# Evictions of q, k and V grouped by engine, V's blocks stored in another order, and GpSimd's row sums in pieces of 256 columns, in a gated pooling and forgetting-attention block

## The chip, the cores and the metric

The kernel runs on one core of a Trainium2 chip. A core has a matrix engine (TensorE, PE in the profile; its weight loads are shown apart as PEld), a vector engine (VectorE, DVE), an engine for activation functions and copies (ScalarE, ACT), a general one (GpSimd, POOL) and a queue engine that issues transfers (SyncE, SP). They run side by side and wait for each other by semaphores; each works through its own queue in order. The metric is the device time of one execution in microseconds (us).

## The reference

One decoder block on 1040 tokens (16 meta tokens in front of 1024), width 1024, eight heads of 64, everything in float32. Cut to what matters here:

```python
h = rmsnorm(x, norm_g)
proj = jnp.einsum('bld,dn->bln', h, w_in)
u_pool, z_pool, q, k, v, z_attn, f_logit, g_pool, g_attn = jnp.split(proj, _split_points(), axis=-1)
y_pool = causal_multiscale_pool(u_pool, pool_w, pool_scale) * jax.nn.silu(z_pool)
log_f = jax.nn.log_sigmoid((f_logit + b_forget).astype(jnp.float32))
y_attn = forgetting_attention(q, k, v, log_f).reshape(B, L, ATTN_WIDTH) * jax.nn.silu(z_attn)
merged = (jax.nn.sigmoid(g_pool) * jnp.einsum('blc,cd->bld', y_pool, w_up_pool)
          + jax.nn.sigmoid(g_attn) * jnp.einsum('blc,cd->bld', y_attn, w_up_attn))
return x + jnp.einsum('bld,de->ble', merged, w_out)
```

and a last RMS norm. Attention is causal softmax with a bias from the running sum of the log forget gates:

```python
s = jnp.einsum('bqhd,bkhd->bhqk', qb, kb).astype(jnp.float32) * scale
s = s + c[:, :, q0:q1, None] - c[:, :, None, :q1]
p = jax.nn.softmax(jnp.where(valid, s, -jnp.inf), axis=-1)
outs.append(jnp.einsum('bhqk,bkhd->bqhd', p.astype(vb.dtype), vb))
```

## The kernel before

**Numbers in two parts.** Matrix products keep nearly float32 accuracy: each operand is split into a high part in a rounded format (written by ACT as a copy) and a low part, the rest (a subtraction on DVE, or on GpSimd for weights), and a product is three matmuls: high by high, high by low, low by high (`g_mm3`, L166 to L172). So every projection that is used again leaves its PSUM bank twice: ACT copies the high part out, then DVE reads the same bank, subtracts the high part and writes the low one.

**Stages.** By the profile's times: to about 54 us the tokens are normed and transposed, and the projections q, k and v of head pair 0 are made, in pieces of the tokens (L479 to L510). To about 83 us the forget gates are made (`gates`, L519). To about 433 us runs attention. Then come a stage of recombined gate projections (L1209 to 1225), the two up-projections (from L1262) and the output product with the last norm (to L1454).

**Attention.** Eight heads stand in four pairs p = 0 to 3, with e = 0, 1 in a pair, and two halves of 512 queries: sixteen units. A unit goes over key blocks b of 128 keys: 5 blocks in the first half, 9 in the second. The keys are stored with the meta tokens in front; block 8 is the last 128 of the 1040 keys and counts only the 16 that block 7 has not. For a block, `qk` (L693) makes the scores in a PSUM bank, ACT and DVE take them out with the gate bias and mask (L713, L717) into a buffer S, and a running maximum is kept (L720, L722). When a unit's blocks are done, `maxes` finds the maxima. Then `soft` (L743) subtracts them (DVE, L749), takes the exponential (ACT, L750), splits it into ph (ACT, L757) and pl (DVE, L758), and GpSimd adds the exponentials of the blocks into acc (L761 to L766), from which the softmax's denominators are summed later. `av` (L770) multiplies two blocks behind by V (L774). The scores of the next unit are interleaved with the softmax of this one.

**Filling.** Between these steps, TensorE's queue is filled with projections of later pairs and with others that are stored to memory for later (class `Fill`). `F.pull(ns)` emits so many nanoseconds' worth of matmuls by a modelled cost, at each place where TensorE would otherwise wait. The generators `f_q`, `f_k` and `f_v` make q, k, V of the next pair with `q_piece` (L265), `k_piece` (L286), `v_piece` (L298) and `v_blocks` (L307). A weight chunk is loaded and split by `split_w` (L148; ACT at L157, GpSimd at L159).

**V.** `v_piece` lets ACT copy a projection to VT, channels by tokens (L301). `v_blocks` transposes blocks of 128 tokens of VT on TensorE (L312) into a bank, and takes them out into V[p, e], a tile of nine blocks with a place for the high and the low part (ACT L321, DVE L322), one head after the other. For pair 0 the blocks 6, 7, 8 and 0 are transposed after the gates (L819), for the other pairs in the filling (L815). As V is stored in the order 0 to 8, the blocks 6 to 8 and block 0 don't lie side by side, and each is an operation of its own.

**What sets the order.** TensorE's queue is in the order in which the program is written (`manual_schedule`, L89). Up to L517 all engines' queues keep the written order among themselves; behind that the framework's planner orders the queues of ACT, DVE, GpSimd and SP by the order written and by modelled times, and it can put later work into gaps of the earlier stage. `after` and `behind` (L113, L118) add an order by hand. Banks for scores and transposes come from `third` (L176): two of a pool and one of another in turn; banks for filling from a pool of two.

**Grouping.** `EVAC` (L42) says how the evictions of q and k are written: for pair 0 both heads together (all ACT copies, then all DVE subtractions), for the other pairs one head after the other. For q, the high part is written to both halves of the partitions.

Of the kernel before, what the change touches and what calls it, by code (L numbers as in the profile page):

```python
# [10 lines left out]
AF = mybir.ActivationFunctionType  # L11
# [11 lines left out]
KB = 128  # L23
NB = 9
# [16 lines left out]
NRC = 2  # L41
EVAC = (((0, 1),), ((0,), (1,)))  # L42
WARM = (4, 0)


def r32(ap):
    return ap.bitcast(F32)
# [7 lines left out]
def tile_hybrid_block(ctx, tc, x, meta, norm_g, w_in, b_forget, pool_w, pool_scale,  # L55
# [209 lines left out]
    def q_piece(p, w, c0, c1):  # L265
# [9 lines left out]

        for group in EVAC[p > 0]:
            for e in group:
                hi(e, rows(e)[0])
                if not p:
                    hi(e, rows(e)[1])  # L280
            for e in group:
                lo(e)
                if p:
                    hi(e, rows(e)[1])

    def k_piece(p, w, t0, t1):  # L286
        ps = yield from g_proj(w, t0, t1)
        for group in EVAC[p > 0]:
            for e in group:
                a, o = rows(e)  # L290
                for c, d in keys_of(t0, t1):
                    nc.scalar.activation(KA[p, e][a, d], ps[a, c], AF.Copy)
            for e in group:
                a, o = rows(e)
                for c, d in keys_of(t0, t1):
                    nc.vector.tensor_tensor(KA[p, e][o, d], ps[a, c], r32(KA[p, e][a, d]), op=ALU.subtract)  # L296

# [8 lines left out]

    def v_blocks(p, *parts):  # L307
        pt = (fill_bank() if spare[0] else third(psS, "ps")).rearrange("p (n e d) -> p n e d", e=2, d=64)
        n = 0
        for b0, b1 in parts:  # L310
            for b in range(b0, b1):
                nc.tensor.transpose(pt[:, n], VT[p][:, KS[b]:KS[b] + KB], ident)  # L312
                n += 1
                yield 109.0
        for e in range(2):
            n = 0
            for b0, b1 in parts:
                pv = pt[:, n:n + b1 - b0]
                n += b1 - b0
                vh = V[p, e][:, b0:b1, e, :]  # L320
                nc.scalar.activation(vh, pv[:, :, e, :], AF.Copy)  # L321
                nc.vector.tensor_tensor(V[p, e][:, b0:b1, 1 - e, :], pv[:, :, e, :], r32(vh), op=ALU.subtract)  # L322

# [12 lines left out]
    def f_v(p):  # L336
        w = w_chunk(COL_V + p * 128)
        VT[p] = gp.tile([128, L], F32, name="vt", tag="g")
        v_alloc(p)
        for c0, c1 in PIECES:  # L340
            yield from v_piece(p, w, c0, c1)
            if c0:
                yield from v_blocks(p, {384: (1, 3), 768: (3, 6)}[c0])

# [134 lines left out]
    for n, (kind, t0, t1) in enumerate(todo):  # L479
# [29 lines left out]
        if n in (4, 7, 10):  # L509
            run(v_blocks(0, (max(1, 2 * (n // 3) - 2), 2 * (n // 3))))  # L510
    G_.close()
# [161 lines left out]
    class Unit:  # L673
# [69 lines left out]
        def soft(self, b):  # L743
# [17 lines left out]
            if b == 1:  # L761
                if c0:
                    nc.gpsimd.tensor_copy(acc[:, :c0], S0[:, :c0])
                accs.append(nc.gpsimd.tensor_tensor(acc[:, c0:], S0[:, c0:], s[:, c0:], op=ALU.add))
            elif b > 1:
                accs.append(nc.gpsimd.tensor_tensor(acc[:kb, c0:], acc[:kb, c0:], s[:kb, c0:], op=ALU.add))  # L766
            if b >= LAG:
                self.av(b - LAG)

        def av(self, b):  # L770
            kb, c0 = self.kb[b], self.c0[b]
            v = V[self.p, self.e][:kb, b].rearrange("p j d -> p (j d)")
            for i, r in enumerate(self.P.pop(b)):
# [36 lines left out]
    def pair_fill(p):  # L810
        if p < 4:
            F.add(f"q{p}", f_q(p))
            F.add(f"k{p}", f_k(p), apart=True)
            F.add(f"v{p}", f_v(p), 4 * p - 2)
            F.add(f"v{p}", v_blocks(p, (6, 9), (0, 1)), 4 * p - 2, apart=True)  # L815

    pair_fill(1)
    gates()
    run(v_blocks(0, (6, 9), (0, 1)))  # L819
    def sums_at(i, tr):  # L820
# [662 lines left out]
```

## Time and profile before

| | us |
|---|---|
| median of three runs | 724.83 (724.09 to 724.98) |
| the profiled execution, whole | 725.36 |
| its span from the first to the last instruction | 723.7 |
| TensorE busy | 709.6 |
| VectorE busy | 515.9 |
| ScalarE busy | 425.4 |
| GpSimd busy | 333.1 |

A row of the timeline gives the start and length in us, the engine, the line of the kernel, the operation, output and inputs with their shapes, how many neighbouring instructions are merged in it, and in square brackets the time that the engine stood idle before it and what ended that. A row of waits gives who waited for whom, with the total in us, how often, and the longest. Matmuls are pipelined, so that the lengths of neighbours overlap; a group of eight has one start and one length.

### The profile page before, as it was taken

What the parts mean: (1) busy time and instruction counts of PE and PEld (TensorE: products, weight loads), DVE (VectorE), ACT (ScalarE), POOL (GpSimd) and SP (SyncE); (2) the same over time, 40 slices, a digit from 0 to 9 for tenths busy, and PEclk for the clock granted to TensorE, in tenths of its full rate; (3) what the DMA queues carried; (4) which work ended last, traced back from release to release, by engine and by line L of the source; (5) the groups of instructions that cost most, each with busy time, mean ns of one, the idle gap of its engine ahead of it and who ended that gap; (6) DMA issues with size and microseconds to landing.
All of it is one profiled execution on the core that took longest, in us unless ns stands there. A gap on an engine that the chain in (4) does not pass through costs nothing.

```text
span 723.7 us, 10860 instructions
## 1 busy us (share of the span) xinstructions
PE 709.6 (98%) x3613; PEld 610.1 (84%) x3613; DVE 515.9 (71%) x917; ACT 425.4 (59%) x944; POOL 333.1 (46%) x417
## 2 busy tenths in 40 slices
PE   9999999999999999999999999999999999999996
PEld 6997899998889888898788788888888888888885
DVE  5743477586788868688586876888847645888775
ACT  7652578666877777776577623446545433525445
POOL 5412145755585756546278632347952010006152
PEclk9999999999999999999999999999999999999998
DMA  9211115886969696695798989599407367761006
GB/s 309 62 28 32 51 52 191 225 277 155 303 205 254 169 257 194 154 254 145 213 276 227 213 273 309 185 293 313 133 29 253 127 222 240 244 251 60 0 1 232
DMA packets 97226, 134.08 MB, mean 185 GB/s; under 512 B 11569, under 2 KB 62769, under 8 KB 94914
## 3 DMA queue, kind: packets, MB, share of 16 engines
q1 hardware_dynamic: 83296, 94.07, 40.5%
q0 software_dynamic: 2512, 18.35, 13.7%
q10 hardware_dynamic: 11362, 20.98, 8.0%
q8 instruction: 28, 0.46, 0.3%
q14 instruction: 28, 0.23, 0.1%
HBM read 103.29 MB, written 62.59 MB: 229 GB/s over the span
## 4 chain that ended last, share of the span: by engine, by line
PE 85%; DVE 4%; ACT 4%; issue 1%; ACTq 0%; POOLq 0%; POOL 0%; DVEq 0%
PE pj L171 48%; PE pj L1043 12%; PE pj L1363 8%; PE po L774 4%; PE pt L1043 4%; PE pt L1363 2%; PE ps L709 2%; PE ps L708 2%; PE pj L528 1%; DVE pl L758 1%; PE pj L709 1%; PE pj L708 1%; DVE ql L273 1%; ACT qa L269 1%; ACT ph L757 1%
## 5 line engine op out<-in xcount | busy, mean ns | idle before, releaser
L171 PE MATMUL pj<-hh,whi 128*128 128x512 f32 (+3 forms) x576 | 128.0, 349 | 0.3 <-DVE ka L296 0.2
L171 PE MATMUL pj<-hh,wlo 128*128 128x512 f32 (+3 forms) x576 | 127.1, 346 | 0.2 <-POOL wlo L446 0.2
L171 PE MATMUL pj<-hl,whi 128*128 128x512 f32 (+3 forms) x576 | 127.3, 346 | 0.0
L159 POOL TENSOR_TENSOR wlo<-raw,whi 128x256 fp32r<-128x256 f32 x100 | 73.8, 767 | 80.5 <-ACT whi L157 34.0
L171 PEld LDWEIGHTS pj<-hh,whi 128*128 128x128 f32 x576 | 97.5, 190 | 11.0 <-PE pj L171 0.5
L171 PEld LDWEIGHTS pj<-hh,wlo 128*128 128x128 f32 x576 | 96.6, 188 | 10.3 <-POOL wlo L446 0.5
L171 PEld LDWEIGHTS pj<-hl,whi 128*128 128x128 f32 x576 | 96.7, 189 | 9.6
L758 DVE TENSOR_TENSOR pl<-S,ph 128x512 fp32r<-128x512 f32 (+4 forms) x112 | 84.4, 764 | 20.3 <-ACT ph L757 19.5
L766 POOL TENSOR_TENSOR acc<-acc,S 128x272 f32<-128x272 f32 (+4 forms) x80 | 76.2, 953 | 28.3 <-ACT S L750 23.1
L1005 POOL TENSOR_TENSOR gw<-graw,gw 128x256 fp32r<-128x256 f32 x52 | 50.6, 996 | 50.2 <-ACT gw L1000 43.3
L1043 PE MATMUL pj<-gh,gw 128*128 128x512 f32 x276 | 64.2, 389 | 0.0
L1043 PEld LDWEIGHTS pj<-gh,gw 128*128 128x128 f32 x276 | 51.8, 188 | 10.8
L722 DVE TENSOR_TENSOR pt<-pt,S 128x400 f32<-128x400 f32 (+2 forms) x96 | 46.5, 484 | 17.1 <-ACT S L713 14.8
L750 ACT ACTIVATE S<-S 128x512 f32<-128x512 f32 (+4 forms) x112 | 50.0, 479 | 12.9 <-DVE S L749 12.9
L757 ACT ACTIVATE ph<-S 128x512 fp32r<-128x512 f32 (+4 forms) x112 | 53.2, 483 | 3.3 <-PE po L774 1.3
L749 DVE TENSOR_TENSOR S<-S,pt 128x512 f32<-128x512 f32 (+4 forms) x112 | 50.1, 500 | 0.7
L1256 DVE TENSOR_TENSOR rl<-pj,rl 128x512 f32<-128x512 f32 x32 | 22.0, 690 | 27.8 <-PE pj L171 27.3
L1000 ACT ACTIVATE gw<-graw 128x512 fp32r<-128x512 f32 x38 | 23.8, 627 | 29.0 <-PE pj L1043 8.0
L774 PE MATMUL po<-pl,V 128*128 128x512 f32 (+4 forms) x112 | 38.1, 340 | 1.3 <-DVE pl L758 1.0
L713 ACT ACTIVATE S<-ps,negc 128x16 f32<-128x16 f32 (+4 forms) x65 | 33.0, 514 | 8.4 <-PE ps L709 7.5
L774 PE MATMUL po<-ph,V 128*128 128x512 f32 (+4 forms) x112 | 36.5, 326 | 0.2 <-ACT ph L757 0.2
L1363 PE MATMUL pj<-opw 128*128 128x512 f32 (+1 forms) x168 | 36.2, 374 | 0.0
(250 smaller groups left out, 1394.8 us busy)
## 6 DMA issues: line engine op xcount, KB each, us to landing
raw<-in_w_in_dram SPq DMA_DIRECT2D x27, 512.0 KB, 7.0
gs<-gs POOLq DMA_DIRECT2D x4, 1536.0 KB, 12.1
graw<-gs SPq DMA_DIRECT2D x12, 512.0 KB, 6.6
gs<-in_w_in_dram ACTq DMA_DIRECT2D x5, 1024.0 KB, 11.8
td<-in_w_out_dram ACTq DMA_DIRECT2D x5, 1024.0 KB, 10.5
graw<-in_w_in_dram SPq DMA_DIRECT2D x9, 512.0 KB, 5.5
xt<-in_x_dram SPq DMA_DIRECT2D x8, 512.0 KB, 7.3
accd<-acc SPq DMA_DIRECT2D x16, 256.0 KB, 3.2
```

What stands on the lines that cost most here:

```text
L159: ins = nc.gpsimd.tensor_tensor(lo[:, k:k + 2], raw[:, k:k + 2], r32(hi[:, k:k + 2]), op=ALU.subtract)
L171: nc.tensor.matmul(ps, a, b, start=(i == 0), stop=(i == len(seq) - 1))
L722: nc.vector.tensor_tensor(m[:kb, c0:], m[:kb, c0:], s[:kb, c0:], op=ALU.max)
L749: nc.vector.tensor_tensor(s[:kb, c0:], s[:kb, c0:], self.pm[:kb, c0:], op=ALU.subtract)
L750: exps.append(nc.scalar.activation(s[:kb, c0:], s[:kb, c0:], AF.Exp))
L757: nc.scalar.activation(ph[:kb, c0:], s[:kb, c0:], AF.Copy)
L758: dves.append(nc.vector.tensor_tensor(pl[:kb, c0:], s[:kb, c0:], r32(ph[:kb, c0:]), op=ALU.subtract))
L766: accs.append(nc.gpsimd.tensor_tensor(acc[:kb, c0:], acc[:kb, c0:], s[:kb, c0:], op=ALU.add))
L774: nc.tensor.matmul(self.po[:, c0:], v, r[:kb, c0:], start=(b == 0 and i == 0), stop=(b == self.nb - 1 and i == 1))
L1005: nc.gpsimd.tensor_tensor(op[:, 1, k:k + 2], raw[:, k:k + 2], r32(op[:, 0, k:k + 2]), op=ALU.subtract)
L1043: nc.tensor.matmul(ps, stat(n, i, p, k), op_h[n][q][k // 2][:, k % 2], start=fresh and m == 0, stop=m == 11, skip_group_check=True)
L1363: nc.tensor.matmul(ps, pick(A_, k, p)[:, i * 128:(i + 1) * 128], pick(B_, k, q)[:, c0:c1], start=start and n == 0, stop=n == 11, skip_grou ...
```

## The change

Four things change.

- The evictions of q and k are written in one way for all pairs: all ACT copies of both heads, then all DVE subtractions. `EVAC` is gone. For pair 0 nothing changes.
- `v_blocks` takes its blocks as a list, and V is stored in the order 1, 2, ..., 8, 0 (`v_at`), so that 6, 7, 8, 0 lie side by side. One ACT copy per head and one DVE subtraction per head take the whole group out, ACT's two first. `av` looks V up by the new place.
- For pair 0 the blocks 6, 7, 8, 0 are transposed and taken out ahead of the gates instead of behind them.
- GpSimd's sums over the blocks are made in operations of at most 256 columns; 512 columns are two operations, 400 are 256 and 144, 272 are 256 and 16.

```diff
-        for group in EVAC[p > 0]:
-            for e in group:
-                hi(e, rows(e)[0])
-                if not p:
-                    hi(e, rows(e)[1])
-            for e in group:
-                lo(e)
-                if p:
-                    hi(e, rows(e)[1])
+        for e in range(2):
+            hi(e, rows(e)[0])
+            hi(e, rows(e)[1])
+        for e in range(2):
+            lo(e)
...
+    def v_at(b):
+        return (b - 1) % NB
+
+    def v_blocks(p, *blocks):
         pt = (fill_bank() if spare[0] else third(psS, "ps")).rearrange("p (n e d) -> p n e d", e=2, d=64)
-        n = 0
-        for b0, b1 in parts:
-            for b in range(b0, b1):
-                nc.tensor.transpose(pt[:, n], VT[p][:, KS[b]:KS[b] + KB], ident)
-                n += 1
-                yield 109.0
+        for n, b in enumerate(blocks):
+            nc.tensor.transpose(pt[:, n], VT[p][:, KS[b]:KS[b] + KB], ident)
+            yield 109.0
+        n, a0 = len(blocks), v_at(blocks[0])
+        hi = [V[p, e][:, a0:a0 + n, e, :] for e in range(2)]
         for e in range(2):
-            n = 0
-            for b0, b1 in parts:
-                pv = pt[:, n:n + b1 - b0]
-                n += b1 - b0
-                vh = V[p, e][:, b0:b1, e, :]
-                nc.scalar.activation(vh, pv[:, :, e, :], AF.Copy)
-                nc.vector.tensor_tensor(V[p, e][:, b0:b1, 1 - e, :], pv[:, :, e, :], r32(vh), op=ALU.subtract)
+            nc.scalar.activation(hi[e], pt[:, :n, e, :], AF.Copy)
+        for e in range(2):
+            nc.vector.tensor_tensor(V[p, e][:, a0:a0 + n, 1 - e, :], pt[:, :n, e, :], r32(hi[e]), op=ALU.subtract)
...
-                accs.append(nc.gpsimd.tensor_tensor(acc[:, c0:], S0[:, c0:], s[:, c0:], op=ALU.add))
-            elif b > 1:
-                accs.append(nc.gpsimd.tensor_tensor(acc[:kb, c0:], acc[:kb, c0:], s[:kb, c0:], op=ALU.add))
+            for c in (range(c0, 512, 256) if b else ()):
+                c1 = min(c + 256, 512)
+                accs.append(nc.gpsimd.tensor_tensor(acc[:kb, c:c1], (S0 if b == 1 else acc)[:kb, c:c1],
+                                                    s[:kb, c:c1], op=ALU.add))
...
     pair_fill(1)
+    run(v_blocks(0, 6, 7, 8, 0))
     gates()
-    run(v_blocks(0, (6, 9), (0, 1)))
```

`k_piece` is regrouped in the same way as `q_piece`, and `v_blocks` is called with lists of blocks in the other places.

More of the change, by code (lines that the diff above doesn't have):

```diff
@@ L41 @@
 NRC = 2
-EVAC = (((0, 1),), ((0,), (1,)))
 WARM = (4, 0)
@@ L274, in lo @@
                                            op0=ALU.mult, op1=ALU.subtract)
-        for group in EVAC[p > 0]:
-            for e in group:
-                hi(e, rows(e)[0])
-                if not p:
-                    hi(e, rows(e)[1])
-            for e in group:
-                lo(e)
-                if p:
-                    hi(e, rows(e)[1])
+        for e in range(2):
[3 more added lines that the diff above has]
+            lo(e)
     def k_piece(p, w, t0, t1):
         ps = yield from g_proj(w, t0, t1)
[L288 to L296, printed above, removed]
+        for e in range(2):
+            a, o = rows(e)
+            for c, d in keys_of(t0, t1):
+                nc.scalar.activation(KA[p, e][a, d], ps[a, c], AF.Copy)
+        for e in range(2):
+            a, o = rows(e)
+            for c, d in keys_of(t0, t1):
+                nc.vector.tensor_tensor(KA[p, e][o, d], ps[a, c], r32(KA[p, e][a, d]), op=ALU.subtract)
     def v_piece(p, w, t0, t1):
@@ L509, in tile_hybrid_block @@
         if n in (4, 7, 10):
-            run(v_blocks(0, (max(1, 2 * (n // 3) - 2), 2 * (n // 3))))
+            run(v_blocks(0, *range(max(1, 2 * (n // 3) - 2), 2 * (n // 3))))
     G_.close()
```

9 lines of the change are left out of this document (5 added, 4 removed).

## The prediction

> **What bounds the kernel now.** I read the page's busy times first, then the busy time by stretch. The columns of the stretches are from and to, length, and busy us with the number of instructions for PE, PEld, DVE, ACT and POOL, then TensorE's clock, the DMA share and GB/s.
>
> ```profile
> PE 709.6 (98%) x3613; PEld 610.1 (84%) x3613; DVE 515.9 (71%) x917; ACT 425.4 (59%) x944; POOL 333.1 (46%) x417
> ```
> ```profile
> 433.00:553.00 120.00, 120.00 (x529) 98.99 (x528) 89.89 (x93) 57.89 (x90) 65.74 (x68) 1.00 0.69 210
> ```
> ```profile
> 83.00:433.00 350.00, 344.95 (x1824) 304.42 (x1823) 268.07 (x553) 244.63 (x620) 202.95 (x242) 1.00 0.75 208
> ```
>
> TensorE is the bound and its clock is full. The change gives it no instruction more or less, and moves only four transposes. So the time can move only by TensorE's idle time: 350.00 - 344.95 = 5.05 us in the attention stage (83 to 433), nothing in the stage behind it (433 to 553). Whatever ACT, DVE and POOL win or lose is worth something only where TensorE stood still for it. The list of TensorE's own waits names the places (total us, times, longest); the row by itself below is from the waits of all engines.
>
> ```profile
> PE pj L708 <- DVE V L322: 1.5, 1, 1.5
> PE ps L708 <- DVE S L717: 1.3, 2, 1.0
> PE po L774 <- DVE pl L758: 1.0, 2, 0.7
> PE ps L708 <- ACT S L713: 0.4, 1, 0.4
> PE pj L171 <- DVE ka L296: 0.2, 1, 0.2
> ```
> ```profile
> ACT V L321 <- DVE V L322: 7.1, 7, 3.0
> ```
>
> That row shows the mechanism that the change works on. L321 and L322 only read the projection's PSUM bank (L321's copy of e=1 needs nothing that L322 made for e=0), and yet ACT waits for DVE: accesses of two engines to one bank are taken in turn, in the order written. ACT, DVE, ACT, DVE costs a hand-over at each step, and each step stands behind whatever else is in that engine's queue. I go through the edits and ask what TensorE gets at each wait.
>
> **The moved transposes: a new wait.** The blocks 6, 7, 8, 0 of V for pair 0 are transposed after the gates now, in the changed kernel before them, directly behind the last V projection of the first stage. They read VT, which ACT writes from that projection (L301).
>
> ```profile
> 52.29 0.28 ACT L321 ACTIVATE V<-pj 128x128 fp32r<-128x128 f32 x1
> 53.40 1.17 PE L171 MATMUL pj<-hh,wlo 128*128 128x272 f32 x8
> 54.41 1.55 PE L528 MATMUL pj<-hh,wfs 128*16 128x384 f32 x8
> 55.18 1.15 ACT L157 ACTIVATE whi<-raw 128x512 fp32r<-128x512 f32 x2 [2.62 <-DMA raw<-in_w_in_dram]
> 56.24 0.26 ACT L321 ACTIVATE V<-pj 128x128 fp32r<-128x128 f32 x1
> 56.40 0.45 ACT L301 ACTIVATE vt<-pj 128x256 f32<-128x256 f32 x2
> 82.93 0.60 PE L312 MATMUL ps<-ident,vt 128*128 128x128 f32 x4
> ```
>
> The projection ends at 53.40 + 1.17 = 54.57. VT is complete at 56.40 + 0.45 = 56.85, because ACT's queue holds the split of the next weights (L157) ahead of it, and that split waits 2.62 us for its DMA. Today the gate matmuls (L528, from 54.41) cover this. With the transposes in front, the cover is gone and everything on TensorE stands behind them. In the changed kernel the second L321 needs no DVE any more and should run right behind the first, at 52.6, so the L301s come as soon as L157 ends: 55.18 + 1.15 + 0.45 = 56.78. Idle time: 56.78 - 54.57 = 2.2 us. Will L157 still be ahead? It was put there in a gap in which ACT waited for DVE; the gap that is left, from 52.6 to the projection's end at 54.57, is 2 us long, and L157 is 1.15, so I think so. Bounds: 0.45 us (L301 alone) if it is not, 2.4 us if the restart costs some more; taken 2.2. The transposes themselves (0.60 us in the last row) cost the same in either place.
>
> **What leaves unit 0's score stage.** The evictions of those transposes now lie among the first score blocks:
>
> ```profile
> 85.41 0.41 PE L171 MATMUL pj<-hh,whi 128*128 128x272 f32 x2
> 85.57 0.31 ACT L321 ACTIVATE V<-ps 128x192 fp32r<-128x192 f32 x1
> 86.16 0.35 DVE L322 TENSOR_TENSOR V<-ps,V 128x192 fp32r<-128x192 f32 x1
> 86.42 0.34 DVE L717 SCALAR_TENSOR_TENSOR S<-ps,negc,mask 128x128 f32<-128x128 f32 x1
> 86.82 0.34 PE L708 MATMUL ps<-qa,ka 128*128 128x144 f32 x1 [1.00 <-DVE S L717]
> ```
>
> TensorE waits 1.00 us for a bank that L717 frees; L717 stands behind L322, which stands behind ACT's L321. With V evicted 25 us earlier both the queue and the bank that V held are free. Saving: at least the 0.35 of L322 and about 0.35 of the wait for L321, so 0.7 to 1.0; taken 1.0, since a second bank is free as well.
>
> **V of pair 3 (and 1): grouped and merged.** The same eviction, eight operations in turn, holds a bank that the scores need:
>
> ```profile
> 346.53 0.32 ACT L321 ACTIVATE V<-pj 128x192 fp32r<-128x192 f32 x1
> 347.00 0.69 ACT L713 ACTIVATE S<-ps,negc 128x512 f32<-128x512 f32 x1
> 347.59 0.21 ACT L321 ACTIVATE V<-pj 128x64 fp32r<-128x64 f32 x1
> 347.72 0.60 ACT L720 ACTIVATE pt<-S 128x512 f32<-128x512 f32 x1
> 348.58 0.39 PE L171 MATMUL pj<-hh,whi 128*128 128x512 f32 x1
> 350.11 0.22 DVE L322 TENSOR_TENSOR V<-pj,V 128x64 fp32r<-128x64 f32 x1
> 350.47 0.47 PE L708 MATMUL pj<-qa,ka 128*128 128x512 f32 x1 [1.50 <-DVE V L322]
> ```
> ```profile
> 183.00 0.21 DVE L322 TENSOR_TENSOR V<-ps,V 128x64 fp32r<-128x64 f32 x1
> 183.39 0.50 PE L708 MATMUL ps<-qa,ka 128*128 128x512 f32 x1 [0.39 <-ACT S L713]
> ```
>
> The eviction lasts from 346.53 to 350.33. After the change it is two ACT copies of 256 columns and two DVE subtractions of 256. No row has these; by the rows of 192 and 64 columns one ACT copy lies between 0.32 and 0.32 + 0.21 = 0.53, a DVE one between 0.35 and 0.57. I take 0.4 and 0.45, as the fixed part is paid once: 1.7 us without anything between, which frees the bank at 348.2. If L713 and L720 (0.69 + 0.60) still get between the two ACT copies, it is 349.5. TensorE wants the bank at 348.58 + 0.39 = 348.97, so the wait of 1.50 shrinks to between 0 and 0.55; saved 0.95 to 1.50, taken 1.4. The wait of 0.39 at 183.39 comes at the end of such an eviction (bank free at 183.21); saved 0 to 0.39, taken 0.3.
>
> **q and k grouped.** The order on each engine stays as written, only the turns between the two go. The one place where TensorE feels it:
>
> ```profile
> 219.88 0.49 ACT L292 ACTIVATE ka<-pj 64x384 fp32r<-64x384 f32 x1
> 220.40 0.56 DVE L296 TENSOR_TENSOR ka<-pj,ka 64x384 fp32r<-64x384 f32 x1
> 221.10 0.36 PE L171 MATMUL pj<-hh,whi 128*128 128x272 f32 x1 [0.21 <-DVE ka L296]
> ```
>
> With the second ACT copy no longer behind DVE this 0.21 should go: 0 to 0.21, taken 0.2. For q there is nothing to win, as no row of TensorE's waits names L269 or L273.
>
> **GpSimd in 256 columns.** The rows by shape (count, busy us, mean ns, idle before):
>
> ```profile
> L159 POOL TENSOR_TENSOR wlo<-raw,whi 128x256 fp32r<-128x256 f32 x100 | 73.8, 767 | 80.5 <-ACT whi L157 34.0 <-PE pj L171 26.3 <-issue 10.5
> L758 DVE TENSOR_TENSOR pl<-S,ph 128x512 fp32r<-128x512 f32 x48 | 49.6, 1040 | 15.7 <-ACT ph L757 15.3
> L766 POOL TENSOR_TENSOR acc<-acc,S 128x512 f32<-128x512 f32 x24 | 35.3, 1471 | 9.6 <-ACT S L750 8.2
> L749 DVE TENSOR_TENSOR S<-S,pt 128x512 f32<-128x512 f32 x48 | 31.1, 683 | 0.7
> ```
>
> Two operations of 256 are 2 x 767 = 1534 ns against 1471, 0.06 us more, and the 272 and 400 columns get a second operation too. All of it is on an engine that is busy 202.95 of 350 us and for which TensorE waits nowhere in this stage: cost 0. What may be won is on DVE: L758 takes 1040 ns where L749, as wide but with one input in PSUM, takes 683, so 48 x 0.36 = 17 us are spent waiting on something. If that is GpSimd, shorter operations halve it. But TensorE waited for L758 only 1.0 us in all, at two places, so I put 0 in the sum and 0 to 1.0 in the range.
>
> **The sum.** 2.2 - 1.0 - 1.4 - 0.3 - 0.2 = -0.7 us. The profiled execution took 725.36 us (span 723.7 and 1.66 around it), 0.53 over the median of the runs, 724.83. So 724.66 for that execution, and 724.1 us beside the median.
>
> **The rivals.** *The new wait is short.* If L301 comes ahead of L157, the front costs 0.45 for L301 and, as an estimate, as much again for the two hand-overs, 0.9 instead of 2.2: 722.8. For it: the planner orders ACT anew. Against it: the gap of 2 us above.
>
> *GpSimd held DVE.* Shorter holds then take the two waits for L758 (1.0) away: 723.1. For it: 1040 against 683. Against it: the longer of the two waits falls where GpSimd runs L159, which has 256 columns already:
>
> ```profile
> 291.94 3.06 POOL L159 TENSOR_TENSOR wlo<-raw,whi 128x256 fp32r<-128x256 f32 x4
> ```
> ```profile
> 293.72 0.39 PE L774 MATMUL po<-pl,V 128*128 128x272 f32 x1 [0.66 <-DVE pl L758]
> ```
>
> [...]
>
> *ACT's runs get too long (the other side).* At q of pairs 2 and 3 ACT now makes its four copies in one run:
>
> ```profile
> 289.23 1.20 ACT L269 ACTIVATE qa<-pj 64x512 fp32r<-64x512 f32 x2 [0.59 <-DVE ql L273]
> ```
>
> Two take 1.20 today and DVE's turn lets score copies (L713) in between; four take 2.4. A score copy behind them comes up to 1.2 us later, and its bank with it. How much of that the other banks cover no row shows; if it is 0.4, TensorE stands 0.8 us for each of the four pieces, 3.2 us: 727.3. Slower than before begins where a piece costs more than 0.7 / 4 = 0.18 us. Against it: today's waits show slack at these places.
>
> *The bank doesn't come free in time.* The planner may keep L713 and L720 ahead of V's second copy, or give the scores another bank that is late: then of the savings only unit 0's 1.0 and k's 0.2 are left, 2.2 - 1.2 = +1.0: 725.8.
>
> **How the numbers follow.** Forecast 48%, 724.1, with its own range 723.0 to 725.4 (front 2.4 with savings of 1.9, to front 2.0 with 3.1 and a little of L758). Short wait 13%, GpSimd 14%, ACT's runs 13%, bank not free 12%. A measurement of this kernel can tell about 0.2% or 1.45 us from no change, so faster is below 723.4, slower above 726.3. Faster: most of the two first rivals (21 of 27) and 9 from the forecast's low end, 30%. Slower: 10 of ACT's runs, 4 of the rest, 14%. No change: 56%. The range, 722.2 to 726.8, takes in both fast rivals with 0.6 below the lower, and the slow one up to a stall of 0.7 per q piece; about 15% are left out.
>
> **What would show it.** Right: an idle stretch of about 2 us on TensorE before L312 near 54.6, waiting for vt; no wait above 0.3 us in unit 0's scores; no wait at V's eviction of pair 3 near 350; L758 of 512 columns below 1040 ns with TensorE's busy time unchanged. Wrong: vt copied ahead of the weight split; a wait over 0.5 us at L708 behind L269; or an idle sum of the attention stage that is not 2 to 3 us smaller than 5.05.

## The result and the profile after

The changed kernel takes 730.12 us, the median of 4 executions (729.72 to 731.69), beside 724.90 (724.09 to 725.22) for the kernel before on the same chip: a ratio of 1.007, with a 95% interval of 1.0054 to 1.0086. It is slower by 5.2 us where 724.1 was forecast, and lies outside the range. The profiled execution took 729.72 us, with a span of 728.0.

The page of the changed kernel, busy times:

```profile
PE 709.6 (97%) x3613; PEld 612.8 (84%) x3613; DVE 510.3 (70%) x909; ACT 426.0 (59%) x936; POOL 354.3 (49%) x481
```

TensorE does the same work in the same busy time. GpSimd has 64 instructions and 21 us more. The list of TensorE's own waits in the changed kernel (who waits for whom; total us, times, longest):

```profile
PE ps L701 <- DVE S L710: 4.4, 1, 4.4
PE pj L1037 <- ACT st L347: 2.3, 1, 2.3
PE ps L307 <- ACT vt L295: 1.9, 1, 1.9
```

The third row is the front wait of the prediction. The 1.5 at V's eviction and the 1.0 in unit 0's scores have left the list, as forecast. But two waits stand on top that no part of the prediction has: one of 4.4 us inside attention, one of 2.3 us at the start of the gate stage. (L701 is the score matmul that was L708, L1037 the gate projection that was L1044.) Busy time by stretch of the changed kernel, columns as in the prediction:

```profile
83.00:95.00 12.00, 12.00 (x79) 11.85 (x78) 8.18 (x27) 7.76 (x19) 3.11 (x5) 1.00 0.22 66
95.00:175.00 80.00, 75.44 (x446) 72.29 (x444) 55.43 (x120) 54.97 (x142) 47.99 (x68) 0.96 0.56 169
175.00:433.00 258.00, 257.24 (x1302) 223.11 (x1301) 198.05 (x403) 180.78 (x448) 170.79 (x232) 1.00 0.80 217
433.00:553.00 120.00, 117.65 (x518) 96.75 (x517) 87.83 (x89) 57.12 (x89) 67.95 (x70) 1.00 0.71 219
```

From 83 to 95 and from 175 to 433 TensorE hardly stands still any more: 0 and 0.76 us. Nearly all of the attention stage's idle time is now in the 80 us from 95 to 175: 4.56 us, and there the granted clock is 0.96. The gate stage, which had no idle time, has 2.35.

To see where each microsecond is lost or won I took the start of the n-th matmul in a kernel minus the start of the n-th in the kernel before (both have 3613). At 58 the four kernels with the transposes ahead of the gates have four matmuls more behind them that the others make later; as these take about as long as four of the gate matmuls (0.60 us for the four, against 0.70 us), the number there is off by some 0.1. The column gives the time in the kernel before, the number is how late the kernel is there, in us of the profiled executions:

```
time in before               50     58     88    143    150    184    340    352    430    440    end
after                     -0.67  +1.21  -0.40  -0.39  +7.16  +6.12  +4.71  +3.00  +1.69  +4.33  +4.36
after, GpSimd whole       -0.88  +2.70  +1.09  +1.14  +1.08  +0.05  +0.01  -1.70  -1.68  -1.68  -1.65
before, only the pieces   -0.10  -0.10  -0.10  -0.10  +7.15  +6.82  +5.40  +5.40  +4.50  +7.32  +7.32
after, without the move   -0.82  -0.82  -2.31  -2.32  +3.62  +2.63  +1.22  -0.51  -1.39  +2.94  +2.95
evictions alone           -0.80  -0.80  -2.26  -2.25  -2.22  -3.19  -3.24  -4.97  -4.88  -4.88  -4.88
evictions alone, again    -0.63  -0.64  -2.13  -2.15  -2.49  -3.47  -3.48  -5.20  -5.18  -5.18  -5.18
copy to gs later          -1.00  +2.57  +0.95  +1.78  +1.65  +0.62  -1.37  -3.08  -4.05  +0.39  +0.67
last unit whole           -0.67  +2.80  +1.19  +1.20  +7.79  +6.74  +4.78  +3.07  +3.35  +3.35  +3.63
both, without the move    -0.61  -0.61  -2.09  -1.48  -1.84  -2.77  -4.76  -6.49  -6.14  -6.14  -6.14
pieces in last unit only  +0.00  +0.00  -0.04  -0.01  -0.05  -0.38  -0.56  -0.56  -1.79  +3.95  +3.94
pieces in units 4 to 14   -0.99  -0.99  -2.47  -2.48  -2.56  -3.54  -5.47  -7.19  -6.81  -6.81  -6.81
the same, move covered    -0.80  -0.80  -2.65  -2.65  -2.98  -4.01  -5.98  -7.68  -7.36  -7.36  -7.30
```

The first row is the result: -0.67 ahead of the front, +1.88 at the front wait, -1.61 in unit 0, +7.55 between 143 and 150, -1.04 to 184, -1.41 to 340, -1.71 at V of pair 3, -1.31 to 430, and +2.64 at the gate stage: +4.36. The other rows are the experiments below. Each row is one execution: up to 352 the kernel with pieces in the last unit only is written as the kernel before, and its row still shows -0.56 at 340 and 352, so a single step of half a microsecond can be chance.

**The wait near 149.** Here are the two kernels where the scores wait. SPq and ACTq are transfers issued by SP and ACT, the number is the time that the issue took; `st` is the staging buffer of a projection that is stored to memory, `gs` the target of a 1 MB copy of weights that ACT issues in its own queue. First the timeline of the changed kernel:

```profile
129.82 2.83 POOL L158 TENSOR_TENSOR wlo<-raw,whi 128x256 fp32r<-128x256 f32 x4
132.31 0.58 ACTq L745 DMA_DIRECT2D gs<-in_w_in_dram  x1
132.68 0.38 SPq L151 DMA_DIRECT2D raw<-in_w_in_dram  x1
133.16 1.05 SPq L359 DMA_DIRECT2D sp_u<-st  x1
...
147.65 0.49 ACT L357 ACTIVATE st<-pj 128x384 f32<-128x384 f32 x1 [7.41 <-DMA sp_u<-st]
148.03 0.59 ACT L706 ACTIVATE S<-ps,negc 128x400 f32<-128x400 f32 x1
148.66 0.33 DVE L710 SCALAR_TENSOR_TENSOR S<-ps,negc,mask 128x112 f32<-128x112 f32 x1 [7.37 <-ACT S L706]
149.05 0.33 PE L701 MATMUL ps<-qa,ka 128*128 128x144 f32 x1 [4.42 <-DVE S L710]
```

And the timeline of the kernel before:

```profile
129.19 2.80 POOL L159 TENSOR_TENSOR wlo<-raw,whi 128x256 fp32r<-128x256 f32 x4
132.02 0.38 SPq L152 DMA_DIRECT2D raw<-in_w_in_dram  x1
132.50 0.53 SPq L366 DMA_DIRECT2D sp_u<-st  x1
133.22 0.60 ACTq L752 DMA_DIRECT2D gs<-in_w_in_dram  x1
...
143.31 0.49 ACT L364 ACTIVATE st<-pj 128x384 f32<-128x384 f32 x1 [2.61 <-DMA sp_u<-st]
```

Read it from the end. TensorE's scores wait 4.42 us for a bank that VectorE's L710 frees; L710 waits for ACT's score copy L706, and that one stands in ACT's queue behind a copy into `st`, at which ACT has stood 7.41 us; `st` (two buffers) is not free until an earlier store of 192 KB has landed. That store took from its issue to ACT's restart 133.16 to 147.65, 14.5 us; before, 132.50 to 143.31, 10.8. What differs is the order of two issues in two queues: before, the store went out 0.72 us ahead of the 1 MB copy, now 0.85 us behind it. SP's queue has the same order in both; its next weight load waits for GpSimd's split, the store stands behind that load, and the split ends 0.66 us later (132.65 against 131.99). The copy on ACT's queue is 0.91 us earlier. The pieces alone move both: in the kernel before with nothing but the pieces the split ends at 132.94, 0.95 us later than before, and the copy is issued at 132.60, 0.62 us earlier, since there the maxima that lead to the copy reach ACT at 128.84 instead of 129.48 (in the changed kernel, with the pieces too, VectorE's last subtraction of the unit before takes 0.41 us instead of 0.82).

What the order does is seen in the packets that each queue moved from 133 to 137 us (packets, MB, share of the 16 transfer engines). q1 is SP's queue, with the weight load and the store; q10 is ACT's, with the copy; q0 is GpSimd's, with a 1 MB transfer of `hs` that it issued at 131.94 (before) and 132.59 (changed). The kernel before, in which q10 moved nothing yet, and then the changed kernel, in which q0 moved nothing yet:

```profile
q1 hardware_dynamic: 1069, 0.57, 63.7%
q0 software_dynamic: 44, 0.36, 43.2%
```
```profile
q10 hardware_dynamic: 374, 0.77, 68.3%
q1 hardware_dynamic: 190, 0.10, 8.4%
```

From 137 to 142 q0 then keeps 73% of the transfer engines in the kernel before and 88% in the changed one, and SP's queue moves 0.18 and 0.09 MB. So the queue that came first had moved most of its bytes before GpSimd's transfer took over; that what was left of the other had to wait until that was through is my reading of these shares. That a kernel without GpSimd's transfer would not have the wait is not tested.

4.42 us of idle time is less than the 7.55 in the table. The rest, 3.13, is TensorE's clock (third number from the end), in a window of the changed kernel:

```profile
149.00:153.00 4.00, 3.82 (x15) 3.49 (x16) 3.87 (x12) 1.12 (x5) 0.00 (x0) 0.58 0.76 211
```

The granted clock drops to half after the gap; the records put it from 149.64 for 6.83 us, and half the clock costs at most 3.41 in that time.

**The wait at the gate stage.** The timeline of the changed kernel at the end of attention:

```profile
419.52 7.83 POOL L759 TENSOR_TENSOR acc<-acc,S 128x256 f32<-128x256 f32 x6
...
422.87 1.78 DVE L921 TENSOR_TENSOR s<-u 128x1039 f32<-128x1039 f32 x1
...
427.37 0.32 SPq L853 DMA_DIRECT2D accd<-acc  x1
...
429.80 0.45 SPq L781 DMA_DIRECT2D sp_y<-t  x1
...
436.25 0.63 ACT L994 ACTIVATE gw<-graw 128x512 fp32r<-128x512 f32 x1 [10.66 <-DMA sp_y<-t]
436.78 1.07 ACT L347 ACTIVATE st<-pj 128x512 f32<-128x512 f32 x2
437.41 1.20 PE L1037 MATMUL pj<-hh,gw 128*128 128x512 f32 x4 [2.35 <-ACT st L347]
```

And of the kernel before:

```profile
415.76 4.09 POOL L766 TENSOR_TENSOR acc<-acc,S 128x400 f32<-128x400 f32 x4
419.88 0.32 SPq L859 DMA_DIRECT2D accd<-acc  x1
425.24 0.45 SPq L787 DMA_DIRECT2D sp_y<-t  x1
429.26 0.63 ACT L1000 ACTIVATE gw<-graw 128x512 fp32r<-128x512 f32 x1 [5.34 <-DMA sp_y<-t]
```

GpSimd's last six pieces take 7.83 us, 1.3 us each, while VectorE adds rows of 1039 columns for the pool (L921); the last four whole sums took 4.09, mostly before those adds began (418.23 in the kernel before). The store of the sums, `accd`, waits for them at the head of SP's queue (427.37 instead of 419.88), the store `sp_y` stands behind it and four other issues (429.80 instead of 425.24), ACT's split of the gate weights waits for that store 10.66 us, and the copy behind it, L347, holds the bank that TensorE needs. Of the store's 4.56 us, 1.81 are SP's queue, as its data were ready at 427.99 (425.21 before); the rest is the data themselves, with the lag of 1.69 in it. Another 2.43 lie behind the issue, from the store to ACT's restart: 6.45 us against 4.02. Why that flight is longer isn't traced.

### The profile page after: what moved, and what is told of

It reads as the page before. It is cut to its first block, busy times and chain, and to the rows that moved or that the text cites. A ratio compares the mean times of both kernels' runs of the same rounds, so it can differ in the third digit from the quotient of the medians.

```text
span 728.0 us, 10932 instructions
## 1 busy us (share of the span) xinstructions
PE 709.6 (97%) x3613; PEld 612.8 (84%) x3613; DVE 510.3 (70%) x909; ACT 426.0 (59%) x936; POOL 354.3 (49%) x481
## 4 chain that ended last, share of the span: by engine, by line
PE 90%; DMA 3%; DVE 2%; ACT 1%; issue 1%; POOL 1%; POOLq 0%; ACTq 0%
PE pj L170 51%; PE pj L1037 12%; PE pj L1357 8%; PE po L768 5%; PE pt L1037 4%; PE pt L1357 2%; DMA sp_u<-st 2%; PE ps L702 2%; PE ps L701 1%; PE pj L521 1%; PE pt L232 1%; DMA sp_y<-t 1%; DVE s L921 1%; PE pj L702 1%; PE pj L701 1%
## 5 line engine op out<-in xcount | busy, mean ns | idle before, releaser
L759 POOL TENSOR_TENSOR acc<-acc,S 128x256 f32<-128x256 f32 (+2 forms) x128 | 92.7, 743 | 22.6 <-ACT S L743 18.7
L751 DVE TENSOR_TENSOR pl<-S,ph 128x512 fp32r<-128x512 f32 (+4 forms) x112 | 79.7, 726 | 18.4 <-ACT ph L750 18.2
L1037 PE MATMUL pj<-gh,gw 128*128 128x512 f32 x276 | 64.3, 389 | 0.0
L1037 PEld LDWEIGHTS pj<-gh,gw 128*128 128x128 f32 x276 | 51.8, 188 | 10.8
L706 ACT ACTIVATE S<-ps,negc 128x16 f32<-128x16 f32 (+4 forms) x65 | 32.9, 512 | 10.3 <-PE ps L702 9.2
L759 POOL TENSOR_TENSOR acc<-S 128x256 f32<-128x256 f32 (+1 forms) x32 | 26.9, 868 | 21.8 <-ACT S L743 18.1
L136 POOL TENSOR_TENSOR X<-G 128x256 f32<-128x256 f32 x8 | 5.8, 740 | 63.9 <-DVE G L1252 63.9
```

The source lines that it names most:

```text
L751: dves.append(nc.vector.tensor_tensor(pl[:kb, c0:], s[:kb, c0:], r32(ph[:kb, c0:]), op=ALU.subtract))
L759: accs.append(nc.gpsimd.tensor_tensor(acc[:kb, c:c1], (S0 if b == 1 else acc)[:kb, c:c1], s[:kb, c:c1], op=ALU.add))
L1037: nc.tensor.matmul(ps, stat(n, i, p, k), op_h[n][q][k // 2][:, k % 2], start=fresh and m == 0, stop=m == 11, skip_group_check=True)
```

## The experiments

All medians are of the same kind as above; the kernel before measured 725.02 beside the first four, 724.56 beside the next four and 724.97 beside the last three. Edits are against the changed kernel unless another is named.

**GpSimd's sums whole again.**

```diff
-            for c in (range(c0, 512, 256) if b else ()):
...
+                accs.append(nc.gpsimd.tensor_tensor(acc[:, c0:], S0[:, c0:], s[:, c0:], op=ALU.add))
+            elif b > 1:
+                accs.append(nc.gpsimd.tensor_tensor(acc[:kb, c0:], acc[:kb, c0:], s[:kb, c0:], op=ALU.add))
```

> The changed kernel with GpSimd's sums in whole operations again; all else as changed. In the changed kernel's trace two waits are new that no part of the prediction had: 4.42 us near 149 us (ACT waits for the store of U's staging buffer, 14.5 us in flight, with TensorE at half clock for 6.8 us behind it; together 7.5 us of lag) and 2.35 us near 437 us (2.65 us of lag). Theory G (GpSimd's pieces): the pieces end the weight split 0.6 us later, the next weight load and U's store stand behind it in SP's queue and get behind ACT's 1 MB copy of weights; and at the end of attention the pieces each wait for VectorE's long adds. Then both go: 730.1 - 7.5 - 2.65 = about 720. Theory E (evictions): grouping lets ACT reach its 1 MB copy 0.9 us earlier, ahead of U's store, whatever GpSimd does. Then only the second wait goes: about 727.5, with the wait near 149 us still there.

Measured: 722.65 us (722.12 to 724.27), ratio 0.9972, interval 0.9961 to 0.9982. One part of the change made the difference between a gain and a loss: 7.5 us. In the table the jumps at 143 to 150 and at 430 to 440 are both gone, as theory G has it. The median is 2.7 above its 720, which is the size of the pieces' gains that go with them (1.4 us from 184 to 340 and 1.3 from 352 to 430). The timeline of this kernel near 133:

```profile
133.66 0.53 SPq L359 DMA_DIRECT2D sp_u<-st  x1
134.36 0.63 ACTq L745 DMA_DIRECT2D gs<-in_w_in_dram  x1
...
144.39 0.49 ACT L357 ACTIVATE st<-pj 128x384 f32<-128x384 f32 x1 [2.46 <-DMA sp_u<-st]
```

The store is 0.70 us ahead of the copy again, and ACT waits 2.46.

**The pieces alone, in the kernel before** (the same edit the other way round).

> The kernel before with GpSimd's sums in pieces of 256 columns and nothing else. Theory G: both new waits appear, 724.9 + 7.5 + 2.65 = about 735, or 728 to 735 where U's store is only partly late. Theory E: at most the second wait, 725 to 727.5, and no wait over 1.5 us near 149 us.

Measured: 732.59 us (731.24 to 732.69), ratio 1.010, interval 1.0083 to 1.0117. Both waits are there without any of the rest. In this kernel's timeline:

```profile
132.60 0.59 ACTq L752 DMA_DIRECT2D gs<-in_w_in_dram  x1
133.44 1.46 SPq L366 DMA_DIRECT2D sp_u<-st  x1
...
150.06 0.49 PE L708 MATMUL ps<-qa,ka 128*128 128x144 f32 x1 [5.15 <-DVE S L717]
...
440.42 1.20 PE L1044 MATMUL pj<-hh,gw 128*128 128x512 f32 x4 [2.53 <-ACT st L354]
```

The copy is 0.84 us ahead. The table shows gains too: -1.4 between 184 and 340 and -0.9 from 352 to 430. So the pieces are good in the middle of attention and bad at two places.

**Without the move** (V's blocks 6, 7, 8, 0 of pair 0 behind the gates again).

```diff
-    run(v_blocks(0, 6, 7, 8, 0))
     gates()
+    run(v_blocks(0, 6, 7, 8, 0))
```

> The changed kernel with pair 0's blocks 6, 7, 8, 0 of V transposed behind the gates again, grouped and merged as changed. Both theories: the wait of 1.9 us near 54 us goes; of the 1.6 us won in unit 0's scores about half comes back, as four evictions instead of eight lie there. Net 0.9 to 1.9 faster than the changed kernel if the later waits stay, 728.2 to 729.2. If the wait near 149 us hangs on where ACT and SP stand to each other within 1 us, it can change with this shift too; then up to 7.5 us less.

Measured: 728.62 us (727.91 to 729.11), ratio 1.005, interval 1.0035 to 1.0065. The front wait is gone, 1.5 us in the median. Unit 0 wins 1.49 all the same (from 58 to 88), so that gain isn't the move's. Both new waits are in its list too (4.2 and 2.5 us).

**The evictions alone** (without the move, sums whole), run twice.

> The kernel before with the grouped and merged evictions and V's new block order, without the move and without GpSimd's pieces. The lag between the traces of before and after shows what the evictions won: 0.66 in the first stage, some 0.8 to 1.6 in unit 0, 3.9 in the rest of attention. Theory G: all of it stays, 724.9 - 5.8 = about 719. Theory E: the wait near 149 us is here too, 719 + 7.5 = about 726.5.

> The grouping alone once more, beside these two, on the same chip: 720.4 if it is as steady as the four times before showed.

Measured: 720.35 us (720.04 to 720.90), ratio 0.9938, interval 0.9923 to 0.9953; and again 719.91 (719.64 to 720.19), ratio 0.9927, interval 0.9915 to 0.9939. The evictions are the good part: 4.7 and 5.1 us, where theory G had 5.8, read from a trace that also held gains of the pieces. TensorE's largest wait of its own in attention is now for `pl` (list of waits, first of these kernels):

```profile
PE po L767 <- DVE pl L751: 2.2, 3, 0.9
```

**The copy to gs later.** One unit of the first pair issues the copies that wait at its second block at its fourth instead, so that the store goes first.

```diff
-            while b == 1 and puts:
+            while b == (3 if self.p == 0 and self.e == 1 and self.half == 0 else 1) and puts:
```

> The changed kernel, with ACT's 1 MB copy of weights (gs) of unit 2 issued two key blocks later, and nothing else. In the kernels with GpSimd's pieces that copy starts 0.84 us ahead of U's store (132.31 against 133.16 in the changed one), in those without 0.7 us behind it, and the store takes 14.5 us against 10.8. Theory O (the order of the two transfers): the store now comes first and lands in about 11 us, the wait near 149 us and the half clock behind it go, 730.1 - 7.5 = about 722.6. Theory P (the pieces slow the store or ACT in some other way): the wait stays, 729 to 731.

Measured: 726.24 us (722.99 to 732.82, 10 executions in groups near 723, 726 and 732), ratio 1.0048, interval 1.0017 to 1.0079. That is 3.6 above the forecast of theory O. In the profiled execution (726.05) the wait is gone, from 143 to 150 the table has -0.13, and what it lacks is elsewhere: 1.7 more at the front wait and 1.8 more at the gate stage, both with half clock behind them (granted clock 0.57 from 56 to 60 and 0.60 from 432 to 436; see the clock, below). Its timeline:

```profile
134.53 1.08 SPq L359 DMA_DIRECT2D sp_u<-st  x1
135.37 0.61 ACTq L745 DMA_DIRECT2D gs<-in_w_in_dram  x1
...
144.96 0.49 ACT L357 ACTIVATE st<-pj 128x384 f32<-128x384 f32 x1 [1.18 <-DMA sp_u<-st]
```

Nothing but the place of ACT's copies of one unit is changed, and the order of the two decides. In five of the kernels:

```
kernel                     copy issued after the store, us   ACT's wait for the store, us
before                              +0.72                              2.61
after, GpSimd whole                 +0.70                              2.46
copy later                          +0.84                              1.18
after                               -0.85                              7.41
before, only the pieces             -0.84                              7.87
```

The other eight traces agree: where the copy is issued 0.69 to 0.85 us behind the store ACT waits 0.95 to 2.71 us (six kernels), where it is 0.84 and 0.85 ahead 7.15 and 7.87 (two).

The groups are wide apart and the interval reaches from +1.2 to +5.7 us. That the two orders still change places between executions, at a distance of 0.8 us, would explain the uppermost group, but no trace of such an execution is there to show it.

**The last unit's sums whole.**

```diff
-            for c in (range(c0, 512, 256) if b else ()):
-                c1 = min(c + 256, 512)
+            w = 512 if self.p == 3 and self.e == 1 and self.half == 1 else 256
+            for c in (range(c0, 512, w) if b else ()):
+                c1 = min(c + w, 512)
```

> The changed kernel, with GpSimd's sums whole in the last unit alone. Theory L (at the end of attention the pieces stand against VectorE's adds of 1039 columns, six operations in 7.8 us, and SP's queue stands behind the last sum): the last sum ends some 4 us earlier, the wait of 2.35 us near 437 us goes, 730.1 - 2.65 = about 727.5. Rival: the wait comes from the 2 us that everything is late behind the wait near 149 us; then it stays, 730. The wait near 149 us stays in both.

Measured: 728.79 us (726.35 to 729.01), ratio 1.0048, interval 1.0032 to 1.0064. The jump at 430 to 440 is gone from the table (+3.35 and +3.35). In the median only 1.3 us of its 2.6 came back: the gain of the pieces between 352 and 430 goes with them (+0.28 where the changed kernel has -1.31), and the profiled execution (729.01) lost 1.6 more at the front (granted clock 0.57 from 56 to 60; see the clock, below).

**Both repairs, without the move.**

> Grouped and merged evictions and GpSimd's pieces, without the move, with the copy of unit 2 two blocks later and the last unit's sums whole. If theories O and L hold: the trace of the changed kernel without the move stood 2.95 us behind the kernel before, with 5.9 us of lag won near 145 us and 3.6 to 4.3 near 434; without both 2.95 - 5.9 - 4 = -7, about 718. If the pieces won nothing elsewhere: as the grouping alone, 720.4.

Measured: 720.07 us (719.04 to 727.77), ratio 0.9953, interval 0.9924 to 0.9982: eight of ten executions at 719.0 to 720.3, two at 727.3 and 727.8. The median lies between the two forecasts, 718 and 720.4. None of the new waits is left in the profiled execution (719.22). The two long ones are 7.5 us longer, which is the size of the first wait; the two issues still lie 0.85 us apart. That they changed places there is argued, not shown.

**Pieces in the last unit only, in the kernel before.**

> The kernel before, with GpSimd's sums in pieces in the last unit alone. Theory L: only the wait near 435 us appears, 725 + 2.7 = about 727.7. Rival (the wait there is a result of the earlier lag): no change, 725.

Measured: 727.73 us (725.96 to 729.31), ratio 1.0037, interval 1.0027 to 1.0047. This alone makes the second wait, 2.7 us at the gate stage's first matmul, so that wait is no result of the lag. In its table row 5.74 us go between 430 and 440: 2.65 of idle time and some 6.8 us at half clock behind it (granted clock 0.95 from 430 to 434, 0.50 to 438 and 0.70 to 442).

**Pieces in units 4 to 14 only, without the move.** This leaves out the whole first pair of heads, where the two transfers race, and the last unit.

```diff
+            w = 256 if 4 <= 4 * self.p + 2 * self.e + self.half < 15 else 512
```

> Grouped and merged evictions without the move; GpSimd's pieces of 256 columns from pair 1 on and not in the last unit, so that neither pair 0's stage, where the copy and U's store race, nor the end of attention has them; the copy is where it was. If the pieces hurt only by those two places, and shorten the waits for L758's results (0.83 and 0.95 us near 201 and 290 us in the grouping alone, 0.3 and 0.4 with pieces): 720.4 - 1.1 = about 719.2, and no execution near 727. If the pieces hurt elsewhere too: 720.4 or more.

Measured: 718.53 us (718.30 to 718.73), ratio 0.9907, interval 0.9894 to 0.9921. Beside the evictions alone on the same chip it is 1.4 us faster, and its 4 executions lie within 0.4 us. What the pieces give is seen in three fences: its list of TensorE's waits, then the groups by shape (count, busy us, mean ns, idle before) of the evictions alone, then its own:

```profile
PE po L769 <- DVE pl L751: 0.8, 2, 0.4
```
```profile
L751 DVE TENSOR_TENSOR pl<-S,ph 128x512 fp32r<-128x512 f32 x48 | 55.4, 1160 | 14.4 <-ACT ph L750 14.2
```
```profile
L751 DVE TENSOR_TENSOR pl<-S,ph 128x512 fp32r<-128x512 f32 x48 | 49.3, 1031 | 14.6 <-ACT ph L750 14.5
```

VectorE's subtraction of 512 columns takes 1031 ns on average instead of 1160, and TensorE's waits for it fall from 2.2 to 0.8 us. Shorter sums on GpSimd went with shorter subtractions on VectorE; whether VectorE is held there or only runs slower no run shows.

**The same with the move under cover.** The four transposes come inside `gates`, behind its three projections instead of ahead of them.

```diff
                 nc.vector.tensor_copy(fT[:, d], ps[:16, c])
+        run(v_blocks(0, 6, 7, 8, 0))
         F.pull(LATENCY)
```

> The same, with pair 0's transposes of V put behind the gates' projections instead of behind all of the gates: VT is long complete there, and the evictions are done before unit 0's scores. If the move is worth only what it takes out of unit 0 (1.6 us with it, 1.2 with the grouping alone), 0.3 to 0.4 less than the kernel without it: about 718.8; no wait over 0.3 us near 54 us.

Measured: 718.21 us (717.80 to 718.40), ratio 0.9903, interval 0.9889 to 0.9916: the fastest of all, 6.8 us below the kernel before, though only 0.3 below the one without the move, and the two ranges overlap. In its timeline the transposes have no idle time ahead of them:

```profile
61.19 0.60 PE L307 MATMUL ps<-ident,vt 128*128 128x128 f32 x4
```

## Why the prediction was wrong

**The step that failed** is "All of it is on an engine that is busy 202.95 of 350 us and for which TensorE waits nowhere in this stage: cost 0". GpSimd's edit measured +7.5 us (730.12 against 722.65). TensorE's list of waits names only the last link. Behind GpSimd stood SP's queue at two places: a load that waits for GpSimd's split with a store behind it, and a store of GpSimd's sums with another store behind it. Both stores hold buffers that ACT needs, and ACT frees TensorE's banks. No bound of mine reached there, as I bounded GpSimd's edit only by what VectorE gains: "0 to 1.0 in the range". None of the rivals was this mechanism.

**Its price per operation** was off as well. Two pieces were costed at 2 x 767 = 1534 ns by the weight split's row. In the changed kernel's groups by shape:

```profile
L759 POOL TENSOR_TENSOR acc<-acc,S 128x256 f32<-128x256 f32 x72 | 66.5, 944 | 18.3 <-ACT S L743 16.8
```
```profile
L751 DVE TENSOR_TENSOR pl<-S,ph 128x512 fp32r<-128x512 f32 x48 | 45.1, 946 | 15.5 <-ACT ph L750 15.4
```

Two pieces take 2 x 944 = 1888 ns for 1471, 0.42 us more, not 0.06. GpSimd's 354.3 us are 21.2 more than before.

**GpSimd held DVE**, the rival at 14%, was right that shorter operations on GpSimd shorten VectorE's: L758's 1040 ns fell to 946, beside 1152 with GpSimd whole and all else as changed, and only the kernels with pieces there gain between 184 and 340 (1.4 to 2.0 us; those with whole sums 0.0 to 0.2). With the evictions grouped TensorE's waits for it had grown to 2.2 us (the evictions alone), so that there was more to win than the 1.0 by which I had bounded it from the trace before. Another 0.9 to 1.3 us are won between 352 and 430 in the kernels whose last unit is in pieces. They lie between 412 and 418 and are the same wait: in the kernel before, the weight loads of `av` (L774) stand there 0.68 and 0.42 us for L758's results and 0.35 for ACT's, and in the kernel with pieces in the last unit only none of them stands. The list of TensorE's waits, by which I had bounded this, has only 0.36 us of it, as the rest stands with the weight loads. The 2.7 us (1.41 + 1.31) were swallowed by the two new waits (7.55 + 2.64), which leaves the 7.5.

**The evictions** were right in sign and too small. V of pair 3: -1.4 forecast, -1.71 measured. V of pair 1: -0.3, and -0.97 between 150 and 184 with the evictions alone. Unit 0: -1.0, and -1.46 with the evictions alone, so I gave to the move what the grouping does: what goes is the ACT, DVE, ACT, DVE turn in front of L717, wherever V is transposed. Left out altogether were 0.6 to 1.0 us ahead of 50, in the first stage, where pair 0's V evictions are grouped too (the prediction takes in only what its waits named from unit 0 on). The kernel before has this row there, and the changed one no wait at that place:

```profile
41.71 0.66 PE L233 MATMUL pt<-ident,xt 128*128 128x128 f32 x4 [0.49 <-DVE hl L236]
```

Together the evictions gave 4.9 and 5.2 us in the traces, where my terms for them came to 2.9.

**The front wait** came where it was put and for the reason given; the timeline of the changed kernel:

```profile
52.74 1.17 PE L170 MATMUL pj<-hh,wlo 128*128 128x272 f32 x8
54.36 1.15 ACT L156 ACTIVATE whi<-raw 128x512 fp32r<-128x512 f32 x2 [2.29 <-DMA raw<-in_w_in_dram]
55.42 0.44 ACT L295 ACTIVATE vt<-pj 128x256 f32<-128x256 f32 x2
55.83 0.66 PE L307 MATMUL ps<-ident,vt 128*128 128x128 f32 x4 [1.92 <-ACT vt L295]
```

1.92 us for 2.2, since the weights arrived a little earlier. What I missed is the clock: in three kernels the same wait of 1.96 to 2.07 us cost another 1.5 us (the table rises by 3.5 to 3.6 from 50 to 58, where the changed kernel has 1.88), at a granted clock of 0.57 to 0.63 from 56 to 60; the changed kernel has 1.00 from 55 to 62. As a whole the move cost 1.5 us with the pieces and 2.3 without (722.65 against 720.35), for a gain that the trace puts at 0.1.

**The new wait is short**, **ACT's runs get too long** and **the bank doesn't come free in time** did not happen: vt stands behind the weight split, there is no wait at L708 behind L269, and the 1.5 at 350 is gone. The signs named for single places came true. The one that failed was the only sum: the idle time of the attention stage should have been 2 to 3 us smaller than 5.05 and was 5.32 (0 + 4.56 + 0.76). The cures were made, and one new wait undid them.

## What to carry to other kernels

Cutting an engine's operations in two is not free because the bound engine never waits for it: follow each of its results through the queues (a load or store waits for it, and what is queued behind that), and look for pairs of transfers in different queues whose order is decided by less than a microsecond. Price several edits of one change apart and run them apart; here one part gained 5 us, one lost 2, and the third lost 10 in two places while it gained 2.7 elsewhere, and limiting it to where it gains made the fastest kernel. When instructions are moved ahead of a piece of work that covered a latency, put them inside it instead.

## What the runs showed of the hardware

**The clock fell to half behind some waits, and not by their length alone.** In the changed kernel the granted clock was half (0.50) from 149.64 to 156.47 us, 6.83 us, and full (1.00) from 13.11, where its records begin, to there and from there to the last matmul. TensorE's waits and the granted clock behind them, by window:

```
kernel                     TensorE idle, us            granted clock (window, us)
after                      1.92 (53.91 to 55.83)       1.00 (55 to 58), 1.00 (58 to 62)
after, GpSimd whole        2.07 (53.70 to 55.77)       0.63 (56 to 60), 0.70 (58 to 62)
copy later                 2.05 (53.58 to 55.63)       0.57 (56 to 60), 0.78 (58 to 62)
last unit whole            1.96 (53.89 to 55.85)       0.57 (56 to 60), 0.78 (58 to 62)
after                      4.42 (144.63 to 149.05)     0.58 (149 to 153), 0.57 (153 to 157), 1.00 (157 to 161)
after                      2.35 (435.06 to 437.41)     1.00 (437 to 441), 1.00 (441 to 445)
before, only the pieces    2.53 (437.89 to 440.42)     1.00 (440 to 444), 1.00 (444 to 448)
copy later                 2.72 (429.34 to 432.06)     0.60 (432 to 436), 1.00 (436 to 440)
pieces in last unit only   2.65 (431.59 to 434.24)     0.50 (434 to 438), 0.70 (438 to 442), 1.00 (442 to 446)
```

Half clock followed 1.96, 2.05 and 2.07 us at the front, and did not follow 2.35 and 2.53 at the gate stage. So the 2.35 us wait of the changed kernel at the gate stage cost nothing more in clock, the one of 2.72 in the kernel with the later copy cost 1.7 more (4.44 in the table from 430 to 440), and the front wait cost 1.9 us in the changed kernel and 3.5 to 3.6 in the three others. A window of the kernel with GpSimd whole behind its front wait shows the clock:

```profile
56.00:60.00 4.00, 4.00 (x18) 2.02 (x17) 0.76 (x2) 0.66 (x2) 3.68 (x5) 0.63 0.20 55
```

By the clock lost in their windows half clock lasted about 3.4 us at the three fronts (55 to 58 and 58 to 62: 0.84 and 0.70 with GpSimd whole, 0.72 and 0.78 with the later copy, 0.73 and 0.78 with the last unit whole) and about 6.8 with the pieces in the last unit only; that is an estimate. The fall of the changed kernel's clock at 149.64 is 136.53 us behind 13.11, and the falls behind the last matmul are 713.39 behind it there and 706.56 behind the first record in the kernel before: 40, 209 and 207 times 3.413, half of the 6.83. I cut the changed kernel's matmul records in steps of that length. The front wait lies in two steps with 0.16 and 1.76 us of idle time, the wait at the gate stage in two with 1.29 and 1.05, the one of 4.42 in two with 1.61 and 2.82, and only at the end of the last did the clock fall. In the other kernels half clock began, by the same windows, at about 57.0, 56.3, 56.4 and 433.6 (an estimate), and in the 3.41 us before that TensorE was idle 2.07, 2.05, 1.96 and some 2.0 us. That the idle time within a step decides is my reading of these few cases; no run tested it. Why half clock lasted 3.4 us in some cases and 6.8 in others stays open.

**The order of two issues less than 1 us apart moved a landing by 3.7.** Issued 0.85 us behind the 1 MB copy the 192 KB store took 14.5 us, issued 0.72 ahead of it 10.8. The packets of 133 to 137 us above show that the queue that came first moved 0.57 or 0.77 MB and the other nothing or 0.10, and that a third transfer, GpSimd's, then held 73 and 88% of the transfer engines. A third staging buffer, which would untie the two, was not tried.
